# A fused layer with a gated delta mixer: side chains at other distances among the dense products

## The chip, the cores and the metric

The kernel runs on one core of one Trainium2 chip. The metric is the device time of one execution in microseconds (us). The engines are TensorE (PE; its weight loads are shown apart as PEld), VectorE (DVE), ScalarE (ACT), GpSimd (POOL) and SyncE (SP), which issues nearly all DMAs here. Times inside the program come from one profiled execution and are counted from the start of its span.

## The reference, cut to what matters

One layer over 2048 tokens of width 1024, in fp32: a norm with modulation, a mixer (a gated convolution and a gated delta rule with four heads of 128), an output projection, a second norm, a gated FFN and a final norm.

```python
h = adaln(x, g_norm_mix[layer], shift_m, scale_m)
p = h @ w_in[layer]
gate_b, gate_c, h_conv, q, k, v, z, a, bt = jnp.split(p, split_at, axis=-1)
ya = gate_b * causal_depthwise_conv(gate_c * h_conv, conv_w_mix[layer])
...
qkv = jax.nn.silu(causal_depthwise_conv(jnp.concatenate([q, k, v], axis=-1), conv_w_qkv[layer]))
q, k = l2_normalize(q), l2_normalize(k)
beta = jax.nn.sigmoid(bt)
g_dec = -jnp.exp(a_log[layer]) * jax.nn.softplus(a + dt_bias[layer])
o = chunked_gated_delta_rule(q, k, v, g_dec, beta)   # per chunk: inverse of a unit triangular matrix,
                                                     # decay exp(g_i - g_j), state carried over chunks
yb = rms_norm(o, g_dn_out[layer]) * jax.nn.silu(z)
x = x + gate_m * (jnp.concatenate([ya, yb], axis=-1) @ w_out[layer])
h = adaln(x, g_norm_ffn[layer], shift_f, scale_f)
gt, up = jnp.split(h @ w_gate_up[layer], 2, axis=-1)
x = x + gate_f * ((jax.nn.silu(gt) * up) @ w_down[layer])
...
return adaln(x, g_norm_final, shift_o, scale_o)
```

## The kernel before

**Tiling.** The mixer goes over four blocks (0 to 3) of 512 tokens, each of four chunks of 128. The normed input of a block stands transposed in `hTh` and `hTl` (a rounded high part and the rest, so that each fp32 product becomes three). A block has 28 strips of 128 columns of `w_in` (k, q, v and z heads, then twelve strips of the convolution branch), 24 dense products each, and then 192 dense products with `w_out`: 864 in all. Weights come through four buffers `wraw`; ScalarE makes `whi` (L189) and VectorE `wlo` (L191), three strips ahead. The same four buffers also serve the rows of the modulation sums (L250, L254) and the tiles of the second norm (L354).

**Ticks.** All other work of the mixer sits in generators, the side chains. `dmm` counts dense products, and after every sixth it calls `tick`, which moves every chain on whose counter has run out; a chain that yields n sleeps for n ticks. So a `yield n` says how many dense products, at least, stand in TensorE's program between two steps of a chain; the framework's scheduler moves instructions a little after that. Each engine works through its own queue in order, so a step whose input is late holds what is behind it. `drain` runs all chains to their end without dense products between.

**The chains that matter here.**
- `head_chain`: from the columns a and b of the input it makes `g` by a series of some 25 small operations on GpSimd (L632 to L666), sleeps, takes prefix sums of `g` on TensorE (L670 to L672) and the decay matrices `E` (L680 products on GpSimd, L685 on TensorE, L687 exponentials on ScalarE, L688 on GpSimd). Then, head by head, it turns the keys (L610), forms k times k (L704), `kd`, `nk`, `ym` (L696 to L707) and the diagonal 32x32 blocks `Dg` (L714). These go to DRAM and come back in another layout (L723, L728).
- The small inverse: VectorE inverts all the 32x32 blocks at once, column by column, a product (L736) and a difference (L738) for each of 31 columns. The result goes through DRAM (L742, L744) into `X` (L752, 32 operations on GpSimd).
- `level_chain`: two steps that make the inverse of 128x128 from the small one (L768 transposes on VectorE, L770 masks on GpSimd, products L775 and L782, ...). `chunk_chain` carries the state over four chunks, `out_chain` (L890, L895, L901) norms and turns the output, `q_chain` (L817, L818) does the queries, `mix_chain` (L957 to L963) the norm of the convolution branch.
- `second_norm(b)`: for each of four tiles of the block before, a load of the finished rows (L354), the sum of squares (L307), its scale on GpSimd (L301, L302), the scaling (L355), a sleep, and two times four transposes (L360), copies (L362) and stores (L363). It runs four times: in blocks 1 to 3, and for the last block in the FFN.
- `transpose_split`: the transposes (L330) of the next block's rows, which `xblock` loads and norms (L322, L323) when the chain is spawned.

Of the kernel before, what the change touches and what calls it, by code (L numbers as in the profile page):

```python
# [52 lines left out]
def layer_kernel(ctx, tc, x, c, w_ada, b_ada, w_ada_final, b_ada_final, g_norm_mix, g_norm_ffn, g_norm_final,  # L53
# [19 lines left out]
    def dense_ps():  # L73
        return pd.tile([P, 512], F32, name="pd")

    def misc_ps():
        return pm.tile([P, 512], F32, name="pm")
# [14 lines left out]
    def h4(t):  # L92
        return t.rearrange("p (a b) -> p a b", a=4)
# [11 lines left out]
    def spawn(gen, delay=1):  # L105
        side.append([gen, delay])

    def tick():
        for e in list(side):
            e[1] -= 1  # L110
            if e[1] <= 0:
                try:
                    e[1] = next(e[0]) or 1
                except StopIteration:
                    side.remove(e)

    def drain():
        while side:
            tick()

    def dmm(*args, **kw):
        mm(*args, **kw)  # L122
        count[0] += 1
        if count[0] % Q == 0:
            tick()
# [103 lines left out]
    def next_w():  # L229
        fill(PRE + 1)  # L230
        return ready.popleft()
# [11 lines left out]
    def temp(dtype=F32):  # L243
        return temps[0].tile([P, D], dtype, name=temps[1], bufs=temps[2])
# [59 lines left out]
    def sum_squares(t):  # L304
        ss = g0.tile([P, 1], F32, name="ss", bufs=4)
        junk = sp.tile([P, D], mybir.dt.bfloat16, name="ht", bufs=2)
        nc.scalar.activation(junk, t, AF.Square, accum_out=ss)  # L307
        rms_scale(ss, 1, D)
        return ss

    def load_norm(src, pool, name):
        tiles = []
        for _ in load_norm_steps(src, pool, name, tiles):
            pass
        return tiles
# [11 lines left out]
    def transpose_k(tiles, k):  # L327
        ps = misc_ps()
        for i in range(CH):
            nc.tensor.transpose(ps[:, i * P:(i + 1) * P], tiles[i][:, k * P:(k + 1) * P], ident)  # L330
        return ps

    def scale_split(ps, k, gcol, scol, hh, hl):
        ht = sp.tile([P, BLK], F32, name="ht", bufs=2)
        nc.scalar.activation(ht, ps, AF.Identity, scale=gcol[:, k:k + 1], bias=scol[:, k:k + 1])
        nc.vector.tensor_copy(hh[:, k, :], ht)  # L336
        nc.vector.tensor_sub(hl[:, k, :], ht, hh[:, k, :].bitcast(F32))  # L337

    def transpose_split(tiles, gcol, scol, hh, hl):
        for k in range(KD):  # L340
            scale_split(transpose_k(tiles, k), k, gcol, scol, hh, hl)
            yield 2
# [3 lines left out]
    Gm, Sm, Gf, Sf = (g0.tile([P, KD], F32, name=n) for n in ("Gm", "Sm", "Gf", "Sf"))  # L346
# [4 lines left out]
    def second_norm(b):  # L351
        for i in range(CH):
            xt = temp()
            nc.sync.dma_start(xt, x1d[b * CH + i])  # L354
            nc.scalar.activation(xt, xt, AF.Identity, scale=sum_squares(xt))  # L355
            yield 2
            for q in range(2):
                ps = misc_ps()
                for k in range(4):
                    nc.tensor.transpose(ps[:, k * P:(k + 1) * P], xt[:, (q * 4 + k) * P:(q * 4 + k + 1) * P], ident)  # L360
                t = sp.tile([P, BLK], F32, name="ht", bufs=2)
                nc.scalar.copy(t, ps)  # L362
                nc.sync.dma_start(xTd[b][q * 4:(q + 1) * 4, :, i * P:(i + 1) * P].rearrange("k p t -> p k t"), h4(t))  # L363
                yield 1
# [18 lines left out]
    def first_sums(A):  # L383
        pool = actx2.enter_context(tc.tile_pool(name="pA", bufs=1, side="right", reuse_waits="tile"))

        def tiles(n):
            return [pool.tile([P, 4, BLK], F32R, name=n + e) for e in ("h", "l")]

        for n in SUMS[:-1]:
            A[n] = tiles(n)  # L390
        for k in range(4):
            t = pool.tile([P, 4, BLK], F32, name="A22" + "hl"[k % 2])
            a, d, c_, e = (t[:, i, :] for i in range(4))
            for i, (b, kk) in enumerate(((0, k), (0, k + 4), (1, k), (1, k + 4))):
                load_scaled(t[:, i, :], b, kk)
            yield 1
            split_k(A["A11"], k, a)
            split_k(A["A12"], k, d)
            yield 1
            nc.vector.tensor_add(e, c_, e)  # L400
            nc.vector.tensor_sub(c_, a, c_)
            split_k(A["S1"], k, e)
            split_k(A["S3"], k, c_)
            yield 1
            nc.vector.tensor_sub(a, e, a)
            nc.vector.tensor_sub(d, d, a)
            split_k(A["S2"], k, a)
            split_k(A["S4"], k, d)
            yield 1
        A["A22"] = tiles("A22")  # L410
# [47 lines left out]
    with ExitStack() as actx:  # L458
# [4 lines left out]
        hT = [ap_.tile([P, KD, BLK], F32R, name=n) for n in ("hTh", "hTl")]  # L463
        strict_r, gones_r = (ap_.tile([P, P], F32R, name=n) for n in ("strict_r", "gones_r"))

        def cv_tile(shape):
            return ap_.tile(shape, F32, name="cv", bufs=NCV)
# [7 lines left out]
        def xblock(b):  # L475
            return load_norm([x[(b * CH + i) * P:(b * CH + i + 1) * P, :] for i in range(CH)], ap_, "kq")
# [99 lines left out]
        for b in range(NB):  # L576
            hh, hl = hT
            if b:
                spawn(second_norm(b - 1), 4)
# [43 lines left out]
            def head_chain(ps, b=b):  # L623
# [40 lines left out]
                nc.gpsimd.tensor_copy(g_hi, g)  # L664
                g_lo = t16("g_lo")
                nc.gpsimd.tensor_sub(g_lo, g, g_hi.bitcast(F32))  # L666
                yield 7
                ps = misc_ps()
                gf = g.rearrange("p j h -> p (j h)")
                mm(ps[:, 0:16], triu, gf, start=True, stop=True)  # L670
# [61 lines left out]
                for k in range(BASE - 1, 0, -1):  # L732
                    c0 = k // 2
                    n = HB - c0
                    pr = prt[:, :k * n].rearrange("p (s c) -> p s c", c=n)
                    nc.vector.tensor_mul(pr, mq[:, 0:k, k:k + 1].to_broadcast([P, k, n]),  # L736
                                         xq[:, k:k + 1, c0:].to_broadcast([P, k, n]))
                    nc.vector.tensor_sub(xq[:, 0:k, c0:], xq[:, 0:k, c0:], pr)  # L738
                    yield 1
                xc = ap_.tile([P, 2, NH * CH, HB], F32, name="Dg")  # L740
                for e in range(2):
                    nc.sync.dma_start(dx[e].rearrange("a (b s) c -> (a b) s c", s=BASE), xq[e * 64:(e + 1) * 64])  # L742
# [163 lines left out]
            if b:  # L906
                ps_ab = misc_ps()
            proj_ab(ps_ab, range(0 if b else 5, KD))
            spawn(head_chain(ps_ab), 1)
            spawn(q_chain(), 1)  # L910

# [82 lines left out]
            for n in range(2):  # L994
                ns = slice(n * 512, (n + 1) * 512)
                pso = [dense_ps() for _ in range(CH)]
                for kp in range(4):
                    wh, wl = next_w()
                    for t in range(CH):
                        while kp == 2 and len(ybs) <= t:  # L1000
                            tick()
                        if n == 0 and kp == 2 and t == CH - 1:
                            drain()
                            if b + 1 < NB:
                                spawn(transpose_split(xblock(b + 1), Gm, Sm, *hT), 1)
                            else:
                                rctx.close()
                                spawn(first_sums(A), 1)
                        tsl = slice(t * P, (t + 1) * P)
                        for k in range(2):  # L1010
                            kk = (kp % 2) * 2 + k
                            if kp < 2:
                                yh, yl = yah[:, kk, tsl], yal[:, kk, tsl]
                            else:
                                yh, yl = (y[:, kk, :] for y in ybs[t])
                            dmm(pso[t], yh, wh[:, k, :], start=(kp == 0 and k == 0), stop=False)
                            dmm(pso[t], yh, wl[:, k, :], start=False, stop=False)
                            dmm(pso[t], yl, wh[:, k, :], start=False, stop=(kp == 3 and k == 1))
                for t in range(CH):
                    row = b * CH + t  # L1020
                    xr = cv_tile([P, 512])
                    nc.sync.dma_start(xr, x[row * P:(row + 1) * P, ns])
                    yo = cv_tile([P, 512])
                    nc.vector.tensor_mul(yo, pso[t], gate_m[:, ns])
                    nc.gpsimd.tensor_add(xr, xr, yo)
                    nc.sync.dma_start(x1d[row][:, ns], xr)
# [88 lines left out]
    def second_half():  # L1115
        yield from second_norm(NB - 1)
        yield from second_sums()
# [252 lines left out]
    for n, (g, s) in enumerate(items):  # L1370
# [22 lines left out]
        a, b, c_ = dense_ps(), misc_ps(), misc_ps()  # L1393
# [53 lines left out]
```

## Time and profile before

| | |
|---|---|
| median of the runs shown | 2555.41 us (2554.2 to 2555.74, 3 runs) |
| the profiled execution | 2564.55 us |
| its span | 2562.6 us |
| mean granted clock of TensorE | 0.974 |

A window's row gives, for a stretch of the span, its length, then busy us and number of instructions of TensorE, its weight loads, VectorE, ScalarE and GpSimd, then the granted clock of TensorE, the share of the DMA engines and GB/s. A row of waits gives who waited, for whom, the total in us, how often, and the longest. A row of one line gives an operation's number, its shortest, median and longest duration in ns, and the first and last start in us. A row of the timeline begins with start and duration and ends, where the engine was idle before, with that idle time and what ended it.

### The profile page before, as it was taken

The numbers are of one execution on the slowest core, as the hardware profiler recorded it, in microseconds if no ns is written. First come the engines' busy times: TensorE is split into PE (matmuls) and PEld (weight loads), VectorE is DVE, ScalarE is ACT, GpSimd is POOL, SyncE is SP. The second block draws the span as 40 slices with busy tenths as digits, with TensorE's granted clock in tenths as the row PEclk, the third lists the DMA queues.
The fourth block names the chain that finished last, engine by engine and source line by source line (L and its number), as shares of the span: only waits on it lengthen the run. The fifth ranks groups of instructions, "written<-read, shape, count | busy, mean of one in ns | idle before, by whom it ended". The sixth has DMA issues, their size and how long they took to land.

```text
span 2562.6 us, 30993 instructions
## 1 busy us (share of the span) xinstructions
PE 2381.4 (93%) x11243; PEld 1952.6 (76%) x11243; DVE 1726.7 (67%) x2498; ACT 1023.2 (40%) x1768; POOL 760.0 (30%) x876
## 2 busy tenths in 40 slices
PE   5899979999799989998999999999999989999996
PEld 4678767787678867886778888878888867778774
DVE  6887648775587738778565556875555466776665
ACT  3633454234633445337543333533333322332232
POOL 2631354223522344222000000000000146765676
PEclk9999989999999989999999999999999989999998
DMA  7352354524552444316673333853333373333342
GB/s 237 107 136 70 120 158 136 149 92 139 153 127 67 132 115 112 99 62 214 189 233 103 103 107 103 249 162 102 104 103 104 94 264 113 119 119 110 119 136 98
DMA packets 397391, 336.99 MB, mean 132 GB/s; under 512 B 39459, under 2 KB 338732, under 8 KB 397238
## 3 DMA queue, kind: packets, MB, share of 16 engines
q1 hardware_dynamic: 396982, 334.91, 43.3%
q8 instruction: 88, 1.44, 0.2%
q14 instruction: 65, 0.53, 0.1%
q10 hardware_dynamic: 256, 0.10, 0.0%
HBM read 261.55 MB, written 73.41 MB: 131 GB/s over the span
## 4 chain that ended last, share of the span: by engine, by line
PE 50%; DVE 10%; DMA 4%; issue 3%; POOL 3%; ACT 3%; POOLq 0%; SPq 0%; ACTq 0%; DVEq 0%
PE pd L122 31%; PE pm L122 16%; DVE acc L1341 1%; DVE wlo L191 1%; DVE d1024l L1248 1%; DVE acc L1357 1%; DVE cv L935 1%; DMA y<-xT 1%; POOL acc L1358 1%; ACT whi L189 0%; DVE wraw L1272 0%; ACT ht L307 0%; DVE T L1274 0%; POOL ss L302 0%; DMA wraw<-in_w_gate_up_dram 0%
## 5 line engine op out<-in xcount | busy, mean ns | idle before, releaser
L189 ACT CAST whi<-wraw 128x1024 fp32r<-128x1024 f32 x276 | 290.0, 1052 | 481.8 <-PE pd L122 272.2
L191 DVE TENSOR_TENSOR wlo<-wraw,whi 128x1024 fp32r<-128x1024 f32 x273 | 345.3, 1265 | 142.2 <-ACT whi L189 129.4
L122 PE MATMUL pd<-hTh,whi 128*128 128x512 f32 x896 | 366.8, 410 | 1.4 <-DVE hTh L336 1.4
L122 PE MATMUL pd<-hTl,whi 128*128 128x512 f32 x896 | 357.7, 399 | 1.8 <-DVE hTl L337 1.8
L122 PE MATMUL pd<-hTh,wlo 128*128 128x512 f32 x896 | 357.1, 399 | 0.0
L1260 POOL TENSOR_TENSOR wraw<-wraw 128x1024 f32<-128x1024 f32 x22 | 59.8, 2724 | 805.7 <-DMA wraw<-in_w_down_dram 804.5
L122 PEld LDWEIGHTS pd<-hTh,whi 128*128 128x128 f32 x896 | 172.8, 193 | 37.0 <-DVE hTh L336 2.8
L122 PEld LDWEIGHTS pd<-hTh,wlo 128*128 128x128 f32 x896 | 172.3, 192 | 36.9
L122 PEld LDWEIGHTS pd<-hTl,whi 128*128 128x128 f32 x896 | 173.0, 193 | 35.5 <-DVE hTl L337 2.6
L1341 DVE TENSOR_TENSOR acc<-acc,pd 128x512 f32<-128x512 f32 x192 | 130.7, 683 | 72.3 <-PE pd L122 72.1
L1302 POOL TENSOR_TENSOR xl<-ra,xh 128x640 fp32r<-128x640 f32 (+1 forms) x88 | 150.3, 1723 | 55.2 <-ACT xh L1301 43.4
L1184 DVE TENSOR_TENSOR sg<-sg,pd 128x512 f32<-128x512 f32 x44 | 30.2, 687 | 175.3 <-PE pd L122 175.3
L1301 ACT CAST yh<-ra 128x256 fp32r<-128x256 f32 x80 | 32.5, 407 | 239.0 <-PE pd L122 233.2
L1341 DVE TENSOR_TENSOR acc<-acc,pm 128x512 f32<-128x512 f32 x120 | 81.9, 683 | 48.9 <-PE pm L122 48.7
L935 DVE SCALAR_TENSOR_TENSOR cv<-cb,pcb,cv 128x512 f32<-128x512 f32 x144 | 113.5, 788 | 0.9
L122 PE MATMUL pd<-d1024h,xh 128*128 128x512 f32 x224 | 91.1, 407 | 21.4 <-DVE acc L1341 16.8
L1302 POOL TENSOR_TENSOR yl<-ra,yh 128x256 fp32r<-128x256 f32 x80 | 69.3, 881 | 106.0 <-ACT yh L1301 105.6
L122 PE MATMUL pm<-d1024h,xh 128*128 128x512 f32 x240 | 95.7, 399 | 0.4 <-DVE acc L1341 0.4
L122 PE MATMUL pm<-d1024l,xh 128*128 128x512 f32 x240 | 95.3, 397 | 0.0
L122 PE MATMUL pm<-d1024h,xl 128*128 128x512 f32 x240 | 94.8, 395 | 0.0
L122 PE MATMUL pd<-d1024l,xh 128*128 128x512 f32 x224 | 89.8, 401 | 0.8 <-DVE d1024l L1248 0.8
L122 PE MATMUL pd<-d1024h,xl 128*128 128x512 f32 x224 | 89.4, 399 | 0.0
(412 smaller groups left out, 6150.9 us busy)
## 6 DMA issues: line engine op xcount, KB each, us to landing
wraw<-in_w_in_dram SPq DMA_DIRECT2D x112, 512.0 KB
wraw<-in_w_gate_up_dram SPq DMA_DIRECT2D x88, 512.0 KB
ra<-act SPq DMA_DIRECT2D x80, 448.0 KB
act<-S SPq DMA_DIRECT2D x80, 256.0 KB
act<-act SPq DMA_DIRECT2D x68, 256.0 KB
wraw<-in_w_ada_dram SPq DMA_DIRECT2D x32, 512.0 KB
wraw<-in_w_out_dram SPq DMA_DIRECT2D x32, 512.0 KB
wraw<-in_w_down_dram SPq DMA_DIRECT2D x22, 512.0 KB
```

The costliest lines, as they stand in the source:

```text
L122: mm(*args, **kw)
L189: nc.scalar.copy(hi, raw)
L191: (lo_engines.popleft() if lo_engines else nc.vector).tensor_sub(lo, raw, hi.bitcast(F32))
L935: nc.vector.scalar_tensor_tensor(cv, cb[:, t:t + BLK], tap[t], cv, op0=ALU.mult, op1=ALU.add)
L1184: nc.vector.tensor_add(s5[i], s5[i], a[i])
L1248: nc.vector.tensor_sub(lo, raw, hi.bitcast(F32))
L1260: nc.gpsimd.tensor_mul(r, r, gate_f)
L1301: nc.scalar.copy(hi, raw[:, c0:c1, :])
L1302: nc.gpsimd.tensor_sub(lo, raw[:, c0:c1, :], hi.bitcast(F32))
L1341: nc.vector.tensor_add(accs[s, u][:, ns], accs[s, u][:, ns], ps)
L1357: nc.vector.scalar_tensor_tensor(t, t, ss, fin["go_d"], op0=ALU.mult, op1=ALU.mult)
L1358: nc.gpsimd.tensor_add(t, t, fin["so_d"])
```

## The change

Four sleeps are changed and nothing else; every operation stays.

```diff
 def second_norm(b):
             nc.scalar.activation(xt, xt, AF.Identity, scale=sum_squares(xt))
-            yield 2
+            yield 8
...
 def head_chain(ps, b=b):
                 nc.gpsimd.tensor_sub(g_lo, g, g_hi.bitcast(F32))
-                yield 7
+                yield 13
...
                 for k in range(BASE - 1, 0, -1):
...
                     nc.vector.tensor_sub(xq[:, 0:k, c0:], xq[:, 0:k, c0:], pr)
-                    yield 1
+                    if k % 3 == 1:
+                        yield 1
...
                         if n == 0 and kp == 2 and t == CH - 1:
                             drain()
                             if b + 1 < NB:
-                                spawn(transpose_split(xblock(b + 1), Gm, Sm, *hT), 1)
+                                spawn(transpose_split(xblock(b + 1), Gm, Sm, *hT), 4)
```

So the second norm sleeps eight ticks instead of two between a tile's scaling and its transposes, the decay's products come thirteen ticks after the series instead of seven, the small inverse sleeps after 11 of its 31 columns instead of after each, and the next block's transposes start four ticks after their rows are asked for. From L740 on, lines of the new file have a number one higher.

On TensorE in block 1, 42 dense products stand between the turn of the a and b columns (L629) and the products with `g` (L670) before, and 78 now. Where the engines that TensorE waits for work, the order moves as follows.

GpSimd in block 1, at the decay (`lv`, `E`) and the scale of the second norm's tiles (`ss`); before:

```order
L680 TENSOR_TENSOR lv<-ck,g_hi 128x512
L680 TENSOR_TENSOR lv<-ck,g_lo 128x512
L301 TENSOR_SCALAR ss<-ss 128x1
L302 TENSOR_TENSOR ss<-ss,mhalf 128x1
L680 TENSOR_TENSOR lv<-ck,g_hi 128x512
L680 TENSOR_TENSOR lv<-ck,g_lo 128x512
L688 TENSOR_TENSOR E<-E,ck 128x512
L301 TENSOR_SCALAR ss<-ss 128x1
L302 TENSOR_TENSOR ss<-ss,mhalf 128x1
```

and now:

```order
L680 TENSOR_TENSOR lv<-ck,g_hi 128x512
L301 TENSOR_SCALAR ss<-ss 128x1
L680 TENSOR_TENSOR lv<-ck,g_lo 128x512
L302 TENSOR_TENSOR ss<-ss,mhalf 128x1
L688 TENSOR_TENSOR E<-E,ck 128x512 x3
L301 TENSOR_SCALAR ss<-ss 128x1
L302 TENSOR_TENSOR ss<-ss,mhalf 128x1
```

The second tile's scale stood behind six of the decay's eight products and stands behind all but part of the last pair now; the third tile's stood behind the first `E` and stands behind three.

VectorE in block 0, where the small inverse begins (`lv` and `yal` are its product and its matrix, `cv` and `cb` the convolution, `vt` a value head); before:

```order
L736 TENSOR_TENSOR lv<-yal 128x31
L930 COPY halo_511<-pd 128x3
L738 TENSOR_TENSOR yal<-yal,lv 128x31
L933 TENSOR_SCALAR cv<-cb,pcb 128x512
L736 TENSOR_TENSOR lv<-yal 128x30
L976 COPY cb<-uhalo_153 128x2
L935 SCALAR_TENSOR_TENSOR cv<-cb,pcb,cv 128x512
L738 TENSOR_TENSOR yal<-yal,lv 128x30
L935 SCALAR_TENSOR_TENSOR cv<-cb,pcb,cv 128x512
L736 TENSOR_TENSOR lv<-yal 128x58
```

and now:

```order
L736 TENSOR_TENSOR lv<-yal 128x31
L831 TENSOR_TENSOR vt<-pm,sk 128x4x128
L738 TENSOR_TENSOR yal<-yal,lv 128x31
L191 TENSOR_TENSOR wlo<-wraw,whi 128x1024
L736 TENSOR_TENSOR lv<-yal 128x30
L738 TENSOR_TENSOR yal<-yal,lv 128x30
L736 TENSOR_TENSOR lv<-yal 128x58
L738 TENSOR_TENSOR yal<-yal,lv 128x29x2
```

The last convolution's steps stand ahead of the inverse now. Between its first and its last operation there were 13 other instructions of VectorE in block 0 and 39, 34 and 31 in blocks 1 to 3; now there are 6, 29, 22 and 25.

SP in block 1, the loads of `wraw` (L184 weights, L250 a modulation matrix, L354 the second norm's tiles) and the second norm's stores (L363); before:

```order
L354 DMA wraw<-x_1_108 128x1024
L184 DMA wraw<-in_w_in_dram 128x8x128
L363 DMA xT_128<-ht 128x4x128 x2
L250 DMA wraw<-in_w_ada_dram 128x1024
L354 DMA wraw<-x_2_109 128x1024
```

and now:

```order
L354 DMA wraw<-x_1_108 128x1024
L363 DMA xT_128<-ht 128x4x128
L184 DMA wraw<-in_w_in_dram 128x8x128
L250 DMA wraw<-in_w_ada_dram 128x1024
L184 DMA wraw<-in_w_in_dram 128x8x128
L250 DMA wraw<-in_w_ada_dram 128x1024
L354 DMA wraw<-x_2_109 128x1024
```

Between two tiles of the norm there stood one weight and one modulation load, and now there stand two of each.

## The prediction

> **What bounds the kernel now.** I read the page first, then the list of waits of TensorE, then the stretches around the longest of them in the timeline and in windows.
>
> ```profile
> span 2562.6 us, 30993 instructions
> PE 2381.4 (93%) x11243; PEld 1952.6 (76%) x11243; DVE 1726.7 (67%) x2498; ACT 1023.2 (40%) x1768; POOL 760.0 (30%) x876
> ```
>
> TensorE is busy for 93% of the span, and every dense product is there after the change too. So a new spacing of the side chains can only move three things: the stalls of TensorE, the clock that it gets after them, and new stalls. The waits, in total us, times, longest:
>
> ```profile
> PE pm L670 <- POOL g L659: 31.9, 4, 8.6
> PE pm L360 <- ACT wraw L355: 13.5, 8, 3.4
> PE pm L610 <- DVE nk L697: 6.8, 2, 3.4
> PE pm L775 <- POOL lv L770: 3.3, 1, 3.3
> PE pm L895 <- POOL ch L890: 2.3, 1, 2.3
> ```
>
> The first row is the decay of a block: TensorE reaches the product with `g` once a block and finds GpSimd's series for `g` unfinished. The second is the second norm's transposes. Both are lines that the change spaces out.
>
> The stall of block 1 in the timeline, with dense products before and after it (start, duration):
>
> ```profile
> 338.05 0.39 PE L122 MATMUL pd<-hTh,whi 128*128 128x512 f32 x1
> 338.28 0.39 PE L122 MATMUL pd<-hTl,whi 128*128 128x512 f32 x1
> ...
> 347.96 0.61 PE L670 MATMUL pm<-g,ck 128*128 128x16 f32 x2 [8.38 <-POOL g L659]
> ...
> 350.26 0.63 PE L122 MATMUL pd<-hTh,wlo 128*128 128x512 f32 x1
> 350.68 0.63 PE L122 MATMUL pd<-hTh,whi 128*128 128x512 f32 x1
> ```
>
> Starts lie 0.23 us apart before the stall and 0.42 after it. So a tick (six dense products) is 1.4 us, and a long stall is paid again in the clock. The granted clock is the column behind POOL in these windows, one for each block, right behind its stall:
>
> ```profile
> 81.00:89.00 8.00, 8.00 (x29) 6.69 (x30) 3.93 (x5) 5.26 (x7) 7.63 (x9) 0.72 0.12 36
> 348.00:356.00 8.00, 7.64 (x21) 5.94 (x21) 4.81 (x4) 0.02 (x1) 7.92 (x8) 0.56 0.19 66
> 647.00:655.00 8.00, 6.70 (x21) 5.30 (x21) 1.84 (x3) 0.00 (x0) 7.81 (x9) 0.69 0.20 66
> 935.00:943.00 8.00, 6.34 (x17) 4.75 (x17) 0.00 (x0) 0.44 (x1) 7.22 (x10) 0.50 0.00 0
> ```
>
> Busy time by missing clock: 8.00x0.28 + 7.64x0.44 + 6.70x0.31 + 6.34x0.50 = 10.9 us.
>
> **The change part by part, against the profiled 2562.6 us.**
>
> (1) *Decay, 7 to 13 ticks.* Six ticks put 36 more dense products ahead of the `g` products: 36x0.23 = 8.3 us, against waits of 31.9/4 = 8.0. If GpSimd kept its pace nothing would be left. But its pace depends on VectorE:
>
> ```profile
> 77.16 1.08 POOL L652 TENSOR_TENSOR sp_p<-sp_p,sp_z 128x16 f32<-128x16 f32 x1
> 79.03 0.22 POOL L652 TENSOR_TENSOR sp_p<-sp_p,sp_z 128x16 f32<-128x16 f32 x1
> 76.00:79.00 3.00, 0.00 (x0) 0.00 (x0) 2.90 (x5) 0.00 (x0) 2.69 (x4) 0.93 0.84 237
> 79.00:81.00 2.00, 0.09 (x1) 0.09 (x1) 0.00 (x0) 0.00 (x0) 1.48 (x7) 0.50 0.69 182
> ```
>
> The same 128x16 operation takes 1.08 us while VectorE is busy (2.90 of 3.00) and 0.22 while it is idle. The idle time came from the stall; with TensorE running on, VectorE gets the next strip's convolution, and the tail of the series slows. About six of its last operations go from some 0.3 to 0.7 us: a rest of 2.5 us a block. Gain 31.9 - 10 = **22**; bounds 14 (ten operations slowed, a rest of 4.5) and 31.9.
> The Trainium skill, GPSIMD Engine Reference, Specifications, says that GpSimd shares its SBUF interfaces with VectorE and contends with VectorE instructions that have two SBUF inputs. It speaks against this part of the change, and the two rows agree. By it, with each operation of the tail at the slow pace, this term would be the lower bound.
>
> (2) *Clock.* Rests of 2.5 us instead of 8 should leave most of the 10.9 us: **8**; bounds 0 and 10.9.
> The Trainium skill, TensorE: Matmul & The Clock Gate, Part 1, says the clock halves after an idle window of about 3.4 us and comes back after as long a busy one. The steps of 0.42 against 0.23 agree. By it a rest of 2.5 us costs no clock, and the term would be 10.9, the sum below 3 us larger.
>
> (3) *Second norm, 2 to 8 ticks between a tile's load and its transposes.* In block 1 ScalarE stood for 9.8 us on the scale of the second tile, which GpSimd computes behind the decay:
>
> ```profile
> 357.83 1.15 ACT L355 ACTIVATE wraw<-wraw,ss 128x1024 f32<-128x1024 f32 x1 [9.81 <-POOL ss L302]
> ```
>
> The second tile now arrives ten ticks behind the first instead of four, and has 8x1.4 = 11 us until its transposes. That covers 3.4 us waits; but its scale still stands behind seven of GpSimd's `L680` products. I take **8** of the 13.5; bounds 0 and 13.5. Its DMAs (SP, four loads and eight stores) are the same, later.
>
> (4) *Small inverse, a yield at every third column.* It reaches VectorE 20 ticks earlier in the program; against the six of (1) that is 14 ticks net. In the order the level chain's first products (L775) stand 84, 67, 84 and 84 dense products earlier in blocks 0 to 3: 19.3, 15.4, 19.3, 19.3 us. They need GpSimd's mask products (L770) behind the small inverse. First starts, one pair a block:
>
> ```profile
> L770 POOL TENSOR_TENSOR lv<-ym,ck x4: 1287/1291/1300, 194.9 to 213.7; 128x512 f32<-128x512 f32 x4
> L775 PE MATMUL pm<-lv x32: 270/275/275, 211.3 to 219.3; 128*128 128x128 f32 x32
> L770 POOL TENSOR_TENSOR lv<-ym,ck x4: 1257/1472/2278, 488.9 to 493.5; 128x512 f32<-128x512 f32 x4
> L775 PE MATMUL pm<-lv x32: 275/275/430, 490.2 to 505.2; 128*128 128x128 f32 x32
> L770 POOL TENSOR_TENSOR lv<-ym,ck x4: 1282/1288/1636, 776.9 to 788.6; 128x512 f32<-128x512 f32 x4
> L775 PE MATMUL pm<-lv x32: 270/275/348, 785.8 to 794.4; 128*128 128x128 f32 x32
> L770 POOL TENSOR_TENSOR lv<-ym,ck x4: 1289/1292/1627, 1054.1 to 1070.6; 128x512 f32<-128x512 f32 x4
> L775 PE MATMUL pm<-lv x32: 270/275/348, 1067.8 to 1076.4; 128*128 128x128 f32 x32
> ```
>
> Slack behind the first mask product (1.3 us): 15.1, 0, 7.6, 12.4. If the chain kept its distance to TensorE, new stalls would be 4.2, 15.4, 11.7 and 6.9: 38 us. But it need not keep it. VectorE, which runs the chain's products and the inverse, from a block's first copy to the inverse's end (stretch, TensorE, weight loads, VectorE):
>
> ```profile
> 326.60:470.70 144.10, 127.11 (x611) 104.92 (x610) 102.16 (x204) 71.44 (x151) 56.37 (x73) 0.94 0.54 157
> 625.00:758.80 133.80, 114.04 (x553) 93.21 (x552) 93.07 (x196) 70.33 (x150) 55.91 (x74) 0.95 0.50 144
> 914.00:1039.50 125.50, 112.51 (x544) 92.39 (x543) 83.10 (x186) 66.83 (x146) 50.27 (x74) 0.93 0.44 120
> 62.00:177.40 115.40, 100.42 (x488) 82.72 (x487) 100.04 (x196) 61.03 (x134) 55.38 (x64) 0.97 0.41 112
> 365.83 0.16 DVE L930 COPY halo<-pd 128x3 f32<-128x3 f32 x1 [12.96 <-ACT cb L928]
> ```
>
> VectorE idles 42, 41 and 42 us of these stretches in blocks 1 to 3, 15 in block 0; the last row is 13 us of that, the echo of TensorE's and ScalarE's stalls. With some 15 us of idleness left (10 in block 0) the chain comes 26 us earlier (5 in block 0), TensorE by (1) to (3) some 12 (6): 14 nearer in blocks 1 to 3. New stalls: about 5, 3, 2, 1. Term **-11**; bounds -38 and +3.3 (the present wait at L775 gone too).
>
> (5) *Spawn of the next transposes at 4 ticks, and the block's end.* The chain ends some 14 ticks earlier, so the end's waits (L895 above, 2.3) can go, and the fresh norm's tiles have three more ticks. But the chunk products that covered the mixed branch's last strip are gone from there. In the order half of the next block's transposes (L330) now stand together, 36 dense products into the output products in blocks 1 and 2, where they wait if the loaded rows are late. **+1**; bounds -9 (a 2.3 us wait more in each of four blocks) and +9 (as much gained).
>
> (6) *Key and query chains.* They start six ticks later on a VectorE with less idle time behind it; block 0 has only 15 us of idleness to give. The wait at L610, 3.4 us at its longest, comes back in one block more: **-4**; bounds -12 (in all four, less the present ones, rounded up) and 0.
>
> Sum: 22 + 8 + 8 - 11 + 1 - 4 = 24 us. The profiled span would be 2538.6; the runs shown have a median of 2555.41, 7 us under that profile's span, so 2555.4 - 24 = **2531 us**.
>
> **Rivals.**
> *A, slower: the chain behind the small inverse keeps its distance.* For it: the inverse is one queue with a DMA round trip on each side, and block 1 has no slack at all. Against: 40 us of VectorE idleness ahead of it. Gains 22 + 8 + 8 + 1 - 4 = 35; stalls 38; clock behind four such stalls as now, 10.9. Slower by 14: 2569. It decides from about 27 us of new stalls on.
> *B, slower: the second norm holds a weight buffer too long.* Loads, mod rows and norm tiles share four `wraw` buffers, of which the norm now has one for 40 ticks a block instead of 16; in blocks 1 and 2 a modulation sum has another.
>
> ```profile
> 339.45 0.38 SPq L184 DMA_DIRECT2D wraw<-in_w_in_dram  x1
> 348.06 1.23 DVE L191 TENSOR_TENSOR wlo<-wraw,whi 128x1024 fp32r<-128x1024 f32 x1 [3.13 <-ACT whi L189]
> ```
>
> A buffer's round was 349.3 - 339.45 = 9.8 us; two buffers for two loads a strip give a strip per 9.8 us, against 24x0.23 + 0.5 = 6.0. Ten strips lack 38 us, three strips ahead cover 18: 20 a block, 40 in all, 2571. Against: no wait of TensorE for a mixer weight stands in its list now.
> *C, larger gain: nothing comes back.* 31.9 + 10.9 + 13.5 + 3.3 = 60: 2496. For it: the idleness of VectorE; against: block 0.
> *D, the change does not do what it says for the decay:* GpSimd slows as much as TensorE runs on. Term (1) 14, (2) 0, the others as above: 8 us gained, 2547.
>
> **How the numbers follow.** Forecast 0.56 (its own range 2505 to 2546), A 0.16, B 0.06, C 0.12, D 0.10. The range reaches half-way to A and C: 2500 to 2560. About 0.2%, 5 us, is what a measurement of this kernel can tell from no change. Faster: 0.54 + 0.12 + 0.08 + 0.02 of A = 0.76; same 0.06; slower 0.18, from A and B.
>
> **What would show it.** Right: the wait at L670 falls under 3 us a block and the clock in the windows behind it above 0.9; waits at L360 halve; the wait at L775 (one line further down in the new file) stays under 12 us in total. Wrong: waits at L775 of 10 us or more in several blocks with a clock under 0.7 behind them (A); TensorE waiting for `whi` or `wlo` in blocks 1 and 2 (B); a rest at L670 of over 4 us (D).

## The result, and the profile after

The change moves nothing: 2559.58 us against 2558.69 us (medians of 19 runs each), a ratio of 1.0008 with a 95% interval of [0.9999, 1.0016]. The forecast was 2531.

What the change was meant to shorten did get shorter, and a new wait of the same size stands at another place. From the list of TensorE's waits of the kernel after (total us, times, longest):

```profile
PE pm L776 <- POOL lv L771: 36.9, 4, 15.9
PE pm L670 <- POOL g L659: 6.2, 3, 3.3
PE pm L360 <- ACT wraw L355: 5.8, 3, 3.0
PE pm L360 <- DVE kd L696: 3.8, 2, 2.0
```

The wait for `g` fell from 31.9 to 6.2 us and the second norm's from 13.5 to 9.6 (two rows): 29.6 us gained. The level chain's first products (L775 before, L776 now) went from 3.3 to 36.9 us: 33.6 us lost. Block 1's stall in the timeline, with the last dense product ahead of it:

```profile
464.40 0.39 PE L122 MATMUL pd<-hTl,whi 128*128 128x512 f32 x1
480.69 3.78 PE L776 MATMUL pm<-lv 128*128 128x128 f32 x16 [15.90 <-POOL lv L771]
```

TensorE does nothing else in those 15.9 us: the dense products that fill the time elsewhere stand behind L776 in its queue. Why the data are late is read from the first mask product on GpSimd (L771) and the start of block 1 (L536, the a and b columns); the first row is of the kernel before, the others of the kernel after:

```profile
L536 PE MATMUL pm<-hTh,wabs x8: 388/392/397, 321.9 to 325.2; 128*16 128x512 f32 x8
```

```profile
L536 PE MATMUL pm<-hTh,wabs x8: 388/392/397, 326.5 to 329.7; 128*16 128x512 f32 x8
L771 POOL TENSOR_TENSOR lv<-ym,ck x4: 1256/1266/1275, 479.4 to 484.6; 128x512 f32<-128x512 f32 x4
L776 PE MATMUL pm<-lv x32: 275/348/580, 480.7 to 488.3; 128*128 128x128 f32 x32
```

Before, the mask product of block 1 started at 488.9 (shown with term (4)), 167.0 us behind the block's start; now it starts at 479.4, 152.9 behind: 14.1 us earlier. TensorE reached its place 165.0 us behind the start before (490.2 less the stall of 3.3) and 138.3 now (464.8): 26.7 us earlier. The difference, 12.6 us, and the 3.3 that was there make the 15.9. In the same rows of blocks 0, 2 and 3 the data come 0, 12 and 7 us earlier.

The clock, in windows behind the wait for `g` and behind L776 (columns as in the prediction; the granted clock is the third from the end), blocks 0 to 3 each, and then, of the kernel before, behind the wait of 3.3 us at L775 in block 1:

```profile
87.00:95.00 8.00, 8.00 (x38) 6.68 (x38) 8.00 (x9) 7.88 (x11) 7.92 (x7) 1.00 0.46 134
354.00:362.00 8.00, 8.00 (x32) 6.54 (x33) 7.12 (x9) 5.25 (x9) 7.92 (x8) 0.79 0.85 262
653.00:661.00 8.00, 8.00 (x25) 6.49 (x26) 6.21 (x8) 4.89 (x8) 7.92 (x8) 0.59 0.73 224
938.00:946.00 8.00, 7.88 (x38) 6.60 (x38) 1.76 (x4) 1.69 (x3) 7.77 (x10) 1.00 0.59 166
196.00:204.00 8.00, 8.00 (x47) 7.46 (x48) 5.02 (x6) 2.18 (x4) 4.05 (x3) 0.83 0.19 57
481.00:489.00 8.00, 8.00 (x51) 7.91 (x51) 4.23 (x7) 2.10 (x4) 3.41 (x3) 0.72 0.11 33
769.00:777.00 8.00, 7.87 (x45) 7.37 (x46) 2.92 (x6) 2.22 (x3) 3.88 (x4) 0.80 0.09 28
1051.00:1059.00 8.00, 8.00 (x40) 7.37 (x41) 2.41 (x5) 2.22 (x3) 3.63 (x3) 0.72 0.06 17
```

```profile
490.00:498.00 8.00, 7.75 (x36) 7.27 (x37) 8.00 (x10) 1.79 (x3) 5.31 (x4) 0.60 0.13 34
```

Behind `g`, busy time by missing clock is 5.0 us where it was 10.9. Behind L776 it is 7.4 us; of these, 3.1 (7.75 x 0.40) stood behind L775 in block 1 before, where the other three blocks had the full clock. So the clock, too, was won at one place (5.9) and lost at another (4.3).

### The profile page after: what moved, and what is told of

The parts are those of the page before. It is cut to its first block, busy times and chain, and to the rows that moved or that the text cites. A ratio compares the mean times of both kernels' runs of the same rounds, so it can differ in the third digit from the quotient of the medians.

```text
span 2560.2 us, 31016 instructions
## 1 busy us (share of the span) xinstructions
PE 2377.2 (93%) x11243; PEld 1951.9 (76%) x11243; DVE 1736.5 (68%) x2498; ACT 1018.9 (40%) x1766; POOL 768.8 (30%) x876
## 3 DMA queue, kind: packets, MB, share of 16 engines
q1 hardware_dynamic: 396982, 334.91, 43.3%
## 4 chain that ended last, share of the span: by engine, by line
PE 56%; DVE 17%; DMA 8%; POOL 8%; ACT 5%; issue 5%; SPq 0%; POOLq 0%; ACTq 0%; DVEq 0%
PE pd L122 34%; PE pm L122 17%; DVE cv L936 2%; DVE wlo L191 2%; DVE acc L1342 2%; POOL X L753 1%; DVE lv L736 1%; DVE yal L738 1%; DMA wraw<-in_w_ada_dram 1%; ACT whi L189 1%; DVE d1024l L1249 1%; PE pm L776 1%; DMA y<-xT 1%; POOL lv L680 1%; DMA cv<-in_x_dram 1%
## 5 line engine op out<-in xcount | busy, mean ns | idle before, releaser
L936 DVE SCALAR_TENSOR_TENSOR cv<-cb,pcb,cv 128x512 f32<-128x512 f32 x144 | 123.8, 860 | 1.7
L1026 POOL TENSOR_TENSOR cv<-cv 128x512 f32<-128x512 f32 x32 | 45.5, 1433 | 167.7 <-DVE cv L1025 134.0
```

The lines of the kernel that those rows point to most:

```text
L936: nc.vector.scalar_tensor_tensor(cv, cb[:, t:t + BLK], tap[t], cv, op0=ALU.mult, op1=ALU.add)
```

## The experiments

Each ratio is to the kernel before, timed on the same chip, with its 95% interval. "Place" is the number of dense products ahead of the level chain's first products in TensorE's order.

### Which edit brings the new stall: e1, e2, e3

e1 is the change with the small inverse as before; e2 keeps the change whole and sleeps longer behind the inverse; e3 is the kernel before with the small inverse's edit alone.

```diff
# e1, against the change
-                    if k % 3 == 1:
-                        yield 1
+                    yield 1
# e2, against the change (behind the inverse's write-back)
-                yield 14
+                yield 28
# e3, against the kernel before
-                    yield 1
+                    if k % 3 == 1:
+                        yield 1
```

> The change without its small-inverse edit: a yield after every column again, the other three edits (13, 8, 4) kept. The level chain's first products then stand 36 dense products (8.3 us) behind their place in the kernel before, 97 to 120 behind that of the change. Theory T (the small inverse edit put these products in TensorE's queue ahead of their data, and its 36.9 us of stalls ate what the decay and the norm gained): the wait at L775 falls from 36.9 us to under 4, L670 stays near 6 and L360 near 6 to 9, nothing new of more than 8 us in all; about 2530 us, 1.1% faster than before. Rival R (the stalls are set by the block's whole dependency chain, so what goes at one place comes back at another): the wait appears at the block's end (chunk chain L895, L856, output products L1009) or in the next block's start, and the time stays within 0.3% of before, about 2557.

> The change with one number more: 28 ticks instead of 14 between the small inverse's write-back and the X masks, so that the level chain's first products stand exactly where they stood before the change (564, 1368, 2232, 3096 dense products) while the inverse itself stays packed and early on VectorE. Theory T: as e1, the stall at L776 gone (under 4 us), L670 and L360 as in the change; about 2528 us, 1.2% faster than before, and not slower than e1, since the chain's data come up to 14 us earlier than there. Rival R: no gain, within 0.3% of before. Rival P (the packed inverse itself costs, by holding VectorE against the strips' convolutions): slower than e1 by 0.3% or more, with waits of the strip products on VectorE (L818, L930, L192).

> The kernel before with the small-inverse edit alone (a yield at every third column). The level chain's first products stand 120, 44, 82 and 119 dense products earlier than before (27.6, 10, 19, 27 us). Theory T: waits at L776 of 20 us or more in all on top of an unchanged wait at L670 of about 32 us (it lies ahead in the block); block 1 stalls least. The time is 0.5 to 1.2% longer than before, about 2580 us. Rival Q (the chain follows VectorE and would come earlier by itself where the decay's stall leaves VectorE idle): stalls at L776 under 12 us and a time within 0.3% of before or shorter.

Measured: e1 2537.24 us, 0.9908 [0.9891, 0.9925]; e2 2522.29 us, 0.9853 [0.9831, 0.9875]; e3 2604.72 us, 1.0172 [1.0153, 1.0192]. TensorE's waits in e1:

```profile
PE pm L895 <- POOL ch L890: 12.2, 4, 4.3
PE pm L360 <- ACT wraw L355: 11.6, 3, 4.8
...
PE pm L775 <- DVE X L783: 1.2, 3, 0.4
```

in e2 (what is left at L776 is too short to stand among its larger waits):

```profile
PE pm L360 <- ACT wraw L355: 11.9, 3, 4.9
...
PE pm L896 <- POOL ch L891: 2.3, 1, 2.3
```

and in e3:

```profile
PE pm L776 <- POOL lv L771: 47.6, 4, 14.9
...
PE pm L670 <- POOL g L659: 34.1, 4, 9.4
```

Theory T holds in all three on where the stall comes from: with the level chain further back it is gone, and with the small inverse's edit alone it stands in full on top of the old ones (e3 lost more than the 0.5 to 1.2% expected). Rival R is half right in e1 only: there the chain stands six ticks further back than before the change, and 12.2 us of waits turn up at the block's end (L895), more than the 8 us that theory T allowed, and the time is 7 us above its 2530. In e2, at the old place, that wait is what it was before, 2.3. So the place can be wrong on both sides.

e3 also shows what the inverse's yields do on VectorE. Windows from the first operation of block 1's inverse to its last, of the kernel before and of e3, and then of the change and of e1:

```profile
427.40:470.70 43.30, 43.30 (x206) 36.00 (x205) 40.75 (x103) 15.23 (x27) 2.52 (x3) 1.00 0.59 165
```

```profile
442.20:485.70 43.50, 43.50 (x207) 36.10 (x206) 40.73 (x103) 14.27 (x26) 1.82 (x3) 1.00 0.59 165
```

```profile
425.40:463.30 37.90, 36.64 (x169) 30.09 (x168) 35.66 (x93) 12.81 (x25) 1.68 (x3) 1.00 0.62 177
```

```profile
420.30:459.60 39.30, 37.13 (x170) 30.53 (x169) 37.15 (x94) 12.62 (x24) 1.78 (x3) 1.00 0.66 185
```

The third pair is VectorE: 103 instructions before and 103 in e3, in 43.3 and 43.5 us; the windows of blocks 0, 2 and 3 hold 77, 98 and 95 in both. Inside the inverse the edit changes neither the number of VectorE's instructions nor, by more than 0.2 us in block 1, its time. The window did get shorter in the change (93), but it is as short in e1 (94), which has a yield after every column: that is the work of the other edits. In e3 the inverse of block 1 ends 150.5 us behind the block's start, and before it was 148.6. The first mask product comes 1.7 us later in block 1 and 1.3, 2.8 and 1.1 us earlier in blocks 0, 2 and 3, while the level chain's place in TensorE's queue is 44 to 120 dense products (10 to 28 us) earlier.

### The yields against the sleep: e4; a place between: e10

```diff
# e4, against e1
-                yield 14
+                yield 8
# e10, against the change
-                yield 14
+                yield 20
```

> e1 (a yield after every column, with 13, 8 and 4) with one number more: 8 ticks instead of 14 behind the inverse's write-back. Its TensorE queue is that of e2 row for row; VectorE has the same number of other instructions between the first and the last of the inverse's 62 (6, 31, 22, 25 against 6, 30, 22, 25). Theory U (the yields between columns do nothing but space TensorE's queue; VectorE's order comes from the scheduler either way): the same time as e2, 2522 us within 6, and X ready at the same place. Rival P2 (packing helps the chain): 5 us or more above e2, with waits at L775.

> The change with 20 instead of 14 ticks behind the inverse's write-back, between the change and e2. The level chain's first products move back by 36, 19, 36 and 36 dense products (8.3, 4.4, 8.3, 8.3 us). Theory T (each microsecond of place in TensorE's queue takes one off the stall until the data are there, and the data's time does not follow): stalls at L776 from 5.0, 15.9, 6.9, 9.1 to 0, 11.5, 0, 0.8, 12 in all; about 2534 us. Rival (the data come earlier or later with the place): stalls that keep 20 us or more in all, or under 5.

Measured: e4 2523.98 us, 0.9859 [0.9844, 0.9873], the same as e2: theory U holds (e4 differs from e1 in the sleep alone, and its wait at L895 is 2.2 us again). e10 2546.97 us, 0.9945 [0.9927, 0.9963]. The first mask product and the level products of block 1 in e2, and in e10 these with TensorE's waits:

```profile
L771 POOL TENSOR_TENSOR lv<-ym,ck x4: 1260/1274/1656, 473.4 to 477.6; 128x512 f32<-128x512 f32 x4
L776 PE MATMUL pm<-lv x32: 275/275/377, 474.7 to 484.9; 128*128 128x128 f32 x32
```

```profile
L771 POOL TENSOR_TENSOR lv<-ym,ck x4: 1254/1279/1914, 471.1 to 476.5; 128x512 f32<-128x512 f32 x4
L776 PE MATMUL pm<-lv x32: 274/275/580, 472.4 to 482.1; 128*128 128x128 f32 x32
...
PE pm L776 <- POOL lv L771: 13.2, 2, 12.3
...
PE pm L783 <- ACT lv L778: 4.6, 2, 2.5
```

The stalls are 12.3 in block 1 and 0.9 in block 3, and 11.5 and 0.8 were worked out from the places. The data start 155.1 us behind the block's start in e2 (318.3), 153.1 in e10 (318.0) and 152.9 in the change: they do not follow the place there. The time, counted by the ratios, is some 11 us above the 2534 expected. Where the chain's first step is late its next ones are too (L783), which the expectation left out; that is 4.6 us, and the rest is not traced.

### Decay and second norm, each alone: e5, e6, e8

e5 is the kernel before with the decay's 13 ticks, and 8 behind the inverse so that the level chain keeps its place; e8 is the kernel before with the second norm's 8 ticks alone; e6 is e2 with the norm back at 2.

```diff
# e5, against the kernel before
-                yield 7
+                yield 13
...
-                yield 14
+                yield 8
# e8, against the kernel before; e6 is the reverse, against e2
-            yield 2
+            yield 8
```

> The kernel before with the decay's edit alone (13 instead of 7), and 8 instead of 14 ticks behind the inverse's write-back, so that the level chain's first products stand at their old place in TensorE's queue. Theory T: the wait at L670 falls from 31.9 to under 6 us and the clock behind it recovers (about 6 of 10.9 us), against some 4 us of new waits at L704 and L610; about 30 us faster than before, 2530. Rival R: under 12 us faster, since the second norm (still 2 ticks) and the key chains take it back: L360 over 20 us, or L610 and L704 over 12 in all.

> e2 with the second norm's sleep back at 2 ticks. What the norm's edit is worth: by term (3) of the prediction 8 us, so 2530. If the norm's stalls only move (e2 still shows 11.9 us at L360): within 0.15% of e2, 2522. If 2 ticks are better behind the new decay: below 2518.

> The kernel before with the second norm's edit alone (8 instead of 2). Theory G (the waits at L670 and L360 are one wait, for GpSimd's queue: what the one place stops waiting for, the other does, unless both are moved): L670 keeps its 32 us, L360 falls from 13.5 to under 5; the time 0 to 8 us below before, 2551 to 2558, so that the two edits alone (e5: nothing) give far less than the 35 us of both in e2. Rival (each edit brings its own): 25 us or more below before, as the step from e6 to e2 is worth, 2533 or less.

Measured: e5 2560.11 us, 0.9998 [0.9987, 1.0008]; e8 2557.39 us, 0.9983 [0.9968, 0.9998]; e6 2550.09 us, 0.9960 [0.9947, 0.9974], 27 us above e2 by the ratios, where 8 were expected. Theory T's 30 us for e5 was wrong: the decay alone brings nothing, the norm alone next to nothing. The waits in e5, and in e8:

```profile
PE pm L360 <- ACT wraw L355: 48.9, 7, 15.9
...
PE pm L670 <- POOL g L659: 1.4, 1, 1.4
```

```profile
PE pm L670 <- POOL g L659: 41.9, 4, 13.4
```

With the decay's products later, TensorE stands at the second norm's transposes instead (13.5 to 48.9); with the norm later, it stands at `g` (31.9 to 41.9). In this sense the two were one wait: what one place no longer waits for, the other does. GpSimd in block 1 of e5, in the timeline: the first norm tile's scale, the decay's series and products, the second tile's scale; and ScalarE's scaling that waits for it:

```profile
326.45 0.56 POOL L302 TENSOR_TENSOR ss<-ss,mhalf 128x1 f32<-128x1 f32 x1
328.37 0.25 POOL L632 TENSOR_TENSOR ab<-ab 128x32 f32<-128x32 f32 x1 [1.36 <-ACT ab L631]
...
344.32 1.11 POOL L659 TENSOR_TENSOR g<-sp_p,nexpa 128x16 f32<-128x16 f32 x1
...
350.98 1.05 POOL L680 TENSOR_TENSOR lv<-ck,g_lo 128x512 fp32r<-128x512 f32 x1
...
352.39 0.57 POOL L302 TENSOR_TENSOR ss<-ss,mhalf 128x1 f32<-128x1 f32 x1
```

```profile
352.99 1.15 ACT L355 ACTIVATE wraw<-wraw,ss 128x1024 f32<-128x1024 f32 x1 [10.74 <-POOL ss L302]
```

The second tile's scale takes 0.8 us and stands behind 24 us of decay.

### The cause at L360, and more or less of the norm's sleep: e11, e7, e12

e11 is e5 with a scaling that does not wait: the second norm's scale is left out of the result. e7 puts the norm at 12 ticks. e12 is e2 with the scale computed on VectorE and ScalarE.

```diff
# e11, against e5
-            nc.scalar.activation(xt, xt, AF.Identity, scale=sum_squares(xt))
+            sum_squares(xt)
+            nc.scalar.activation(xt, xt, AF.Identity, scale=1.0)
# e7, against e2
-            yield 8
+            yield 12
# e12, against e2
-            nc.scalar.activation(xt, xt, AF.Identity, scale=sum_squares(xt))
+            ss = g0.tile([P, 1], F32, name="ss", bufs=4)
+            junk = sp.tile([P, D], mybir.dt.bfloat16, name="ht", bufs=2)
+            nc.scalar.activation(junk, xt, AF.Square, accum_out=ss)
+            nc.vector.tensor_scalar(ss, ss, 1.0 / D, EPS, op0=ALU.mult, op1=ALU.add)
+            nc.scalar.activation(ss, ss, AF.Sqrt)
+            nc.vector.reciprocal(ss, ss)
+            nc.scalar.activation(xt, xt, AF.Identity, scale=ss)
```

> e5 (decay at 13 alone, the level chain at its old place), where the second norm's scaling on ScalarE runs with the constant 1.0 and does not wait for the tile's scale; GpSimd still computes that scale, unused, so the norm's scaling is left out of the result. Theory G (in e5 TensorE waits at L360 because the second tile's scale stands in GpSimd's queue behind the decay's series and products): the wait at L360 for the scaled tile falls from 48.9 us to under 6, nothing of that size takes its place, and the time is about 2527 us, 33 below e5. Rival (the tile's load or ScalarE's queue is what is late, or the stalls only move): L360 keeps over 20 us, or L670, L610 and L704 take over 20, and the time is above 2545.

> e2 with the second norm's sleep at 12 ticks instead of 8. The three waits at L360 in e2 are 11.9 us in all, 4.9 at the longest, and four ticks are 5.5 us: if the tile's scale is what is late (theory N), they go and the time is 8 to 12 us below e2, 2512. If the waits come from the order of ScalarE's or GpSimd's queue (the scale stands behind the decay's products wherever the transposes are): L360 keeps over 6 us and the time is within 0.2% of e2. If the wraw buffers decide (rival B): TensorE waits for whi or wlo in blocks 1 and 2, and the time is 5 us or more above e2.

> e2 with the second norm's scale taken off GpSimd: mean square and reciprocal on VectorE, square root on ScalarE. Theory G: the 11.9 us at L360 (three waits for the scaled tile) go, at the price of table loads of 1.28 us on ScalarE, which is idle for half of these stretches; 2512 us, 10 below e2. Rival: VectorE's queue, which the convolutions and key products fill there, holds the scale as long as GpSimd's did, and ScalarE's queue waits behind it: L360 keeps 10 us or more and the time is at e2's or above, 2522 to 2535.

Measured: e11 2529.27 us, 0.9860 [0.9844, 0.9876]; e7 2533.62 us, 0.9894 [0.9880, 0.9908]; e12 2518.02 us, 0.9831 [0.9812, 0.9851], the lowest ratio here, 1.7% faster than before. The waits at the norm's transposes (L361 in e11, L366 in e12) and at `g` (L676 in e12), those of e7 last; with the row of e11 goes the second tile's sum of squares in block 1 on ScalarE:

```profile
PE pm L361 <- ACT wraw L356: 19.8, 7, 6.3
345.27 1.06 ACT L307 ACTIVATE ht<-wraw 128x1024 bf16<-128x1024 f32 x1 [3.58 <-DMA xT<-ht]
```

```profile
PE pm L676 <- POOL g L665: 5.8, 4, 2.0
PE pm L366 <- DVE kd L702: 5.0, 3, 1.7
PE pm L366 <- ACT wraw L361: 1.9, 1, 1.9
```

```profile
PE pm L670 <- POOL g L659: 9.7, 4, 3.3
PE pm L704 <- ACT E L687: 8.4, 3, 3.5
PE pm L610 <- DVE kd L696: 7.4, 2, 4.1
PE pm L360 <- ACT junkd L616: 6.5, 3, 4.1
```

e11 has the time that theory G gave (2527), though the wait did not fall under 6: 29 of the 48.9 us were GpSimd's scale, and 19.8 stay, for a scaling that depends on nothing of GpSimd. Here the rival has a part. In block 1, where 6.3 us stay, the sum of squares stood 3.58 us behind a store of `ht`, the buffers that it shares with the norm's transposed copies. In e12 the wait for the scaled tile falls from 11.9 us in e2 to 1.9, but the one for `g` grows from 2.5 to 5.8, and the time is not the 10 us below e2 that were expected: the two intervals overlap. e7 fits none of its three cases: the wait for the scaled tile goes, but waits at `g`, `E` and the keys grow, and the time is 11 us above e2. Eight ticks are the best of the values tried (2, 8, 12).

### The spawn of the next transposes: e9

```diff
# e9, against e2
-spawn(transpose_split(xblock(b + 1), Gm, Sm, *hT), 4)
+spawn(transpose_split(xblock(b + 1), Gm, Sm, *hT), 1)
```

> e2 with the next block's transposes spawned at 1 tick again. By term (5) of the prediction worth 1 us: 2523, within 0.2% of e2. If the spawn is what sets e6 10 us below e5: about 2532, with waits at L330 up by 6 us or more, or a block's end that stalls.

Measured: 2531.95 us, 0.9890 [0.9865, 0.9914], against 0.9853 [0.9831, 0.9875] for e2. The intervals touch, but e5 and e6, which differ by the same edit (and by the inverse's yields, worth nothing by e4), lie 10 us apart too. Its wait for `g`, and VectorE in block 1 where the decay's series (`sp_s`) begins:

```profile
PE pm L670 <- POOL g L659: 15.1, 4, 5.8
```

```profile
333.98 1.28 DVE L254 SCALAR_TENSOR_TENSOR wraw<-wraw,cs 128x1024 f32<-128x1024 f32 x1 [2.32 <-DMA wraw<-in_w_ada_dram]
335.18 0.24 DVE L645 RECIPROCAL sp_s<-sp_s 128x16 f32<-128x16 f32 x1
```

In e9 the reciprocal at the head of the series stands in VectorE's queue behind a modulation sum that waits for its load; in e2 it stands ahead of that sum. The reciprocal starts 16.5 us behind the start of block 1 in e9 and 12.0 in e2, and `g` is ready 31.5 and 25.5 us behind it. The expectation looked for the price at L330 or at the block's end; the wait that grew is at L670, from 2.5 to 15.1 us, while the one for the scaled tile (L360) fell from 11.9 to 3.1.

## Why the prediction was wrong, step by step

**Term (4) failed, and with it the sign.** The step was "It reaches VectorE 20 ticks earlier in the program", from which the chain was to come 26 us earlier in blocks 1 to 3 and 5 in block 0. e3 shows that the yields do not change the number of VectorE's instructions inside the inverse, nor bring its end forward in block 1. The places that the order showed for VectorE (13 other instructions inside the inverse, now 6) were right, but they came with the decay's edit, not with this one: with the decay's edit and no change of the yields, e5's windows from the first to the last operation of the inverse hold 69, 94, 80 and 89 instructions of VectorE, and those of the kernel before 77, 103, 98 and 95. What the chain did gain, 0, 14, 12 and 7 us, it has in e1 too, without this edit, all but some 5 us of block 3 (3, 12, 13 and 2). VectorE's idleness in block 1 fell only from 45 to 27 us of the stretch from the block's start to the inverse's end; I had taken 15. TensorE's own advance of 26.7 us against "some 12" plus the 15.4 of the order was right. New stalls: 33.6 us instead of 11. So the chain did not come nearer with its place, and what was taken from ahead of it on TensorE became a wait. Rival A had the mechanism and the stalls (38 against 36.9), with a chance of 0.16; its condition, "from about 27 us of new stalls on", was met. Its time, 2569, was 10 us too high.

**In times rather than stalls:** all edits but (4), forecast at 35 us, are worth 23.5 in e1 (0.92% of 2559) and 37.6 in e2 (1.47%), where the chain's place is the old one; the place that edit (4) gives the chain costs 25.6 against e1 and 39.7 against e2, instead of 11. Counted from e2, the 26 us between forecast (24) and result (-2) are all term (4): 28.7 more lost there, and 2.6 more gained by the rest. e1 lies 14 us behind e2 because the decay's six ticks push the chain past its old place (L895; e4, with the chain back there, is 12.5 us faster than e1 by the ratios).

**Terms (1) and (3)** had the right sum, 30, for 29.6 us of waits gone, but not as two terms: the prediction gave each a gain of its own, and alone the decay's edit gives nothing (e5) and the norm's some 4 us (e8). The sentence under (3), that the tile's scale "still stands behind seven of GpSimd's products", was the clue; it was not carried to what (1) alone would do. GpSimd's tail did slow, and by more than was taken. From the first L652 to the end of `g` it takes 11.5, 7.7, 8.6 and 7.2 us before and 13.8, 11.4, 12.5 and 10.9 after, 3.4 us more on average. In block 1 VectorE is busy for 6.67 of 7.5 us there (346.5 to 354), where it had 1.85 of 5.0 (343 to 348). Yet only 1.6 us a block are left at L670, not 2.5, because the tail starts 2.4, 1.1 and 3.1 us nearer to the start of blocks 1 to 3; that this makes up for it was luck, and why it starts earlier was not tried. So the rest of 4.5, the lower bound, was not reached. The Trainium skill, GPSIMD Engine Reference, Specifications, names contention of GpSimd with VectorE instructions that have two SBUF inputs. The slower tail agrees with it, though no run here separates that cause.

**Term (2)** forecast 8 and got 5.9 back behind `g` and -4.3 behind L776. The stalls at L776 of 5.0, 15.9, 6.9 and 9.1 us cost 1.4, 2.2, 1.6 and 2.2 us of clock: hardly in proportion. Shorter waits cost as much: behind `g`, 1.7 us in block 1 and 3.3 in block 2, where TensorE had waited 1.54 and 3.30 us; block 0's 1.4 us cost nothing.

```profile
353.83 0.39 PE L670 MATMUL pm<-g,ck 128*128 128x16 f32 x2 [1.54 <-POOL g L659]
652.61 0.57 PE L670 MATMUL pm<-g,ck 128*128 128x16 f32 x2 [3.30 <-POOL g L659]
```

The Trainium skill, TensorE: Matmul & The Clock Gate, Part 1, has the clock halved after an idle window of about 3.4 us until as long a busy one has passed. By it a stall costs, by estimate, half of 3.4, 1.7 us, whatever its length. The four rows behind L776 lie near that. The rows behind `g` do not: 1.7 us were lost behind a wait shorter than that window, and 3.3 behind one as long. So the prediction's reading, that a rest of 2.5 us costs no clock, is not borne out.

**Term (5)** was +1 and is about +9.5 (e9), its upper bound, by a way that I had not seen. **Term (6)**, -4, was about right: the waits at L610, L704 and L817 (L818) grew from 17.0 to 23.3 us (the sums of all their rows). Rival B is out: there is no wait for `whi` or `wlo` of the mixer among TensorE's larger ones. Rival D is out: 6.2 us are left at L670. Rival C's size (60) was never there, but e12 reaches 43.

What stays open: in the two profiled executions the mixer did get longer, and the part behind it shorter. TensorE's last product with `w_out` starts at 1184.9 us before and at 1197.1 after, 12.2 later; from 50 us on up to there, all of TensorE's waits sum to 78.6 us before and 89.3 after. What is left of the span is 1377.7 us before and 1363.1 after. The change reaches that part in one place: the second norm of the last block runs there and sleeps longer there too, and its wait for the scaled tile (2.8 us before, L360 for `y`) is gone. That is little of the 14.6 us, and they do not follow the norm's sleep: the stretch takes 1369.8 and 1376.3 us in e1 and e2, with 8 ticks, and 1366.9 in e3, with 2. TensorE's order differs there as well: before, five products with `A12h` and `A12l` stand ahead of the first with `A11h`, and after the change they follow. What sets this part's time was not tried, so that the change moves nothing is partly luck. In the mixer alone, counted to that product, e1 gains 19.5 us and e2 35.6.

## What to carry to other kernels

A `yield` in a hand-spaced program can move one engine's queue and leave another's alone. Before counting on a chain to come earlier, check on the engine that sets its pace whether its order changes at all; if not, every dense product taken from ahead of its consumer becomes a stall. Two waits of one engine whose data come through the same in-order queue can be one wait: space both, or move one source off that queue, and cost them as one term. Here the change with 28 ticks behind the inverse gives 1.5%; with the norm's scale off GpSimd as well it is 1.7%, though that last step is not clear of the noise.

## What the runs showed of the hardware that was not expected

One small operation in an in-order queue can hold far more than its own time. The scales of the second norm take 0.8 us each; behind the decay on GpSimd they were worth 29 us of TensorE's waits in e5. In block 1 of e9 a reciprocal of 0.24 us stood behind a modulation sum that had waited 2.32 us for a DMA; against the block's start it came 4.5 us later than in e2, and `g` 6 us later.

The clock lost behind a wait of TensorE did not follow the wait's length: in windows of 8 us it was 2.2 us behind a wait of 15.9 us, 1.4 behind one of 5.0, 3.3 behind one of 3.3, 1.7 behind one of 1.5 and nothing behind one of 1.4.
